# Moving the projection of the gated addend from the attention to the gate stage of a two-layer hybrid encoder

## The chip, the cores and the metric

One core of a Trainium2 chip runs the whole kernel. The metric is the device time of one execution in microseconds (us). PE is TensorE, DVE VectorE, ACT ScalarE, POOL GpSimd; SP is SyncE, which here issues every DMA.

## The reference

The kernel does one inference step of a two-layer encoder over 1024 prompt tokens and 64 sample tokens, T = 1088 columns here. Each layer projects the normalized input, runs three token mixers (latent attention with 8 heads, causal pooling, chunk-band attention with 4 heads), merges them with gates, projects out and adds to x. The part of interest is the last line of a layer, in which `ple` is an input of 256 channels that depends on nothing else in the layer:

```python
def trunk_layer(x, ple, ...):
    h = rmsnorm(x, norm_in)
    ...
    m = (gates[..., :D_MODEL] * (o_a @ w_o_mla)
         + gates[..., D_MODEL:2 * D_MODEL] * (o_b @ w_o_pool)
         + gates[..., 2 * D_MODEL:] * (o_c @ w_o_ca))
    x = x + m @ w_out

    x = x + jax.nn.sigmoid(rmsnorm(x, ple_norm) @ w_ple_gate) * (ple @ w_ple_proj)
```

Widths: D_MODEL 1024, `ple` 256, so the projection `ple @ w_ple_proj` gives 1024 channels for 1088 tokens.

## The kernel before, in words

Activations lie channels by tokens: 8 blocks of 128 channels, each cut into two halves of H = 544 tokens, and a half into two quarters of C = 272 columns, which is the width of a matmul. For precision each operand is split into a rounded part and its rest (`split`: ScalarE makes the first, DVE or POOL the second), and one product is three matmuls (`mm3`, L132 to L134).

A layer runs through these stages: the input projection (`gemm`, L404), the attention, first the 4 chunk heads (scores S at L1034, softmax on DVE and ACT, transposes pT at L891, weighted sums pv at L917 and L925), then the 8 latent heads (scores at L1105), the merge, the output projection, and the gate stage (`ple_pairs`, matmuls in `plain`, L372). `plain` takes each of 4 pairs of channel blocks (p and p + 4); for each block and each token half it sums 48 matmuls into one PSUM tile g, calls the pair's `out`, and then its `mid`.

The code is written in program order, which is a priority: at build time a scheduler with an estimated clock per engine puts an instruction that is ready ahead of others that are not, later code filling idle time. What stands in the kernel is the outcome: a fixed queue for each engine, taken in order, with semaphores between. The DMAs all stand in one such queue, SP's.

Beside the attention run generators that are advanced step by step as filler: `ple_proj` (the projection), `pool_branch` (the pooling mixer, tile pbm) and then `merge_bc` (the part of the merge that needs no latent heads, tile mps, multiplied out at L1424). `begin_beside` makes them and the list FIRST = (2, 2, 1) says how many steps of them stand ahead of the first head. `ple_proj` loads `p` and `wpp`, splits them, computes the projection into a PSUM tile pps of pool po, copies it on ScalarE (L1444) to a tile o, and stores o to a DRAM buffer pp_d. In the gate stage `load` reads pp_d back, and `out` takes the sigmoid of the normalized sum (L748, L752; for the first pair L751 scales a copy), multiplies (L754) and adds to x (L755).

## Time and profile before

| what | value |
|---|---|
| three runs | 2278.78, 2288.59 and 2279.34 us |
| median | 2279.34 us |
| the profiled execution | 2290.6 us |
| its span in the trace | 2288.8 us |
| PE busy | 2163.4 us, 95% of the span |
| DVE busy | 1743.5 us, 76% |
| ScalarE busy | 1176.3 us, 51% |
| GpSimd busy | 693.4 us, 30% |
| granted TensorE clock, mean | 0.976 of full |

The span is the time from the first to the last event of one execution on the core; the profiled execution is a little longer than its span, and longer than the median. Busy shares are means over stages of different kinds. In layer 0 the chunk heads run from about 572 to 685 us, the latent heads to 905, the merge to 969, the output projection to 1053 and the gate stage to 1155; in layer 1 the chunk heads from 1706 to 1816 and the gate stage from 2182 to 2283.

### The profile page before, as it was taken

Reading aid. Unit: us, or ns where it says so; the run is one execution under the profiler, and the core shown is the slowest. Engines: PE = TensorE matmul, PEld = TensorE weight load, DVE = VectorE, ACT = ScalarE, POOL = GpSimd, SP = SyncE. Lnnn points to the kernel's source line nnn. Section 1 sums busy time; section 2 is a strip of 40 time slices with the busy share of each in tenths; the row PEclk is TensorE's granted clock in tenths of the full one; section 3 lists DMA queues with packets and bytes.
Section 4 is the critical chain, followed back from the end, with each engine's and each line's share of the span. In section 5 each row is a group of like instructions: output and inputs, shape, how many; then the busy total and the mean of one; then the engine's idle time right before and its main releaser. Section 6 shows DMA issues by size and latency. Waiting matters only on the chain.

```text
span 2288.8 us, 44876 instructions
## 1 busy us (share of the span) xinstructions
PE 2163.4 (95%) x16326; PEld 2083.9 (91%) x16326; DVE 1743.5 (76%) x3590; ACT 1176.3 (51%) x2491; POOL 693.4 (30%) x918
## 2 busy tenths in 40 slices
PE   5999999999789999899989999999988899999998
PEld 4999999999588998899979999999987889998998
DVE  8777888676568889887686678876747788889764
ACT  6234455454667666335453343555546776653341
POOL 0000044676455554000000000547574665430000
PEclk8999999999899999999989999999999999999999
DMA  3534546455966764545634345554569666645472
GB/s 125 185 110 135 185 142 193 129 158 143 279 196 183 198 172 136 204 173 179 210 107 139 118 158 173 165 157 127 159 179 276 199 186 179 186 162 186 144 232 74
DMA packets 222191, 385.81 MB, mean 169 GB/s; under 512 B 30404, under 2 KB 114196, under 8 KB 221972
## 3 DMA queue, kind: packets, MB, share of 16 engines
q1 hardware_dynamic: 221972, 382.95, 54.2%
q8 instruction: 130, 2.13, 0.4%
q14 instruction: 89, 0.73, 0.1%
HBM read 248.16 MB, written 134.70 MB: 167 GB/s over the span
## 4 chain that ended last, share of the span: by engine, by line
PE 62%; DMA 15%; DVE 13%; ACT 4%; issue 3%; POOL 2%; SPq 1%; DVEq 0%; ACTq 0%; POOLq 0%
PE g L404 36%; PE g L372 6%; PE S L1105 3%; PE pv L925 3%; PE pT L891 3%; DMA pp<-o 3%; DMA g<-z 2%; PE mps L132 1%; DMA mb<-g 1%; SPq L87 1%; DVE wop L121 1%; DMA r<-rd 1%; PE mps L134 1%; PE mps L133 1%; PE vps L1074 1%
## 5 line engine op out<-in xcount | busy, mean ns | idle before, releaser
L110 ACT CAST wop<-wraw 128x512 fp32r<-128x512 f32 (+1 forms) x238 | 143.8, 606 | 259.3 <-PE g L404 154.8
L865 POOL TENSOR_SCALAR P<-P,st 128x640 f32<-128x640 f32 (+8 forms) x216 | 155.3, 723 | 203.0 <-DVE st L864 122.3
L121 POOL TENSOR_TENSOR wop<-wraw,wop 128x512 fp32r<-128x512 f32 (+1 forms) x80 | 99.3, 1244 | 382.9 <-ACT wop L110 382.4
L121 DVE TENSOR_TENSOR PT<-pT,PT 128x512 fp32r<-128x512 f32 (+4 forms) x360 | 167.6, 473 | 39.3 <-ACT PT L110 37.3
L121 DVE TENSOR_TENSOR wop<-S,wop 128x512 fp32r<-128x512 f32 x178 | 141.6, 795 | 68.1 <-ACT wop L110 67.6
L110 ACT CAST wop<-S 128x512 fp32r<-128x512 f32 x202 | 124.6, 618 | 123.4 <-PE g L404 119.6
L110 ACT CAST PT<-pT 128x512 fp32r<-128x512 f32 (+4 forms) x360 | 147.0, 420 | 54.4 <-PE pT L891 47.8
L404 PE MATMUL g<-B11h,wop 128*128 128x272 f32 x832 | 152.4, 294 | 16.5 <-ACT B11h L112 12.7
L925 PE MATMUL pv<-PT,V 128*128 128x256 f32 x928 | 165.4, 297 | 2.5 <-DVE PT L121 1.6
L1105 PE MATMUL S<-K,Q 96*128 96x384 f32 (+5 forms) x672 | 158.8, 353 | 6.5 <-ACT P L857 6.5
L132 PE MATMUL mps<-oh,wop 128*128 128x272 f32 x512 | 155.2, 304 | 8.6 <-DVE g L1424 3.9
L891 PE MATMUL pT<-ident,P 128*128 128x128 f32 x936 | 158.5, 279 | 2.9 <-DVE PT L121 1.2
L404 PE MATMUL g<-T3h,wop 128*128 128x272 f32 x832 | 153.9, 293 | 7.7 <-ACT T3h L110 5.0
L404 PE MATMUL g<-B21h,wop 128*128 128x272 f32 x832 | 156.3, 298 | 4.8 <-ACT P L416 4.6
L404 PE MATMUL g<-T1h,wop 128*128 128x272 f32 x832 | 151.7, 293 | 3.6 <-DVE z L681 1.9
L404 PE MATMUL g<-T2h,wop 128*128 128x272 f32 x832 | 152.9, 294 | 2.1 <-ACT T2h L110 1.8
L404 PE MATMUL g<-B22h,wop 128*128 128x272 f32 x832 | 151.0, 293 | 0.0
L404 PE MATMUL g<-T4h,wop 128*128 128x272 f32 x832 | 149.7, 291 | 0.0
L134 PE MATMUL mps<-oh,wop 128*128 128x272 f32 x512 | 148.3, 290 | 0.0
L857 ACT ACTIVATE P<-S,st 128x384 f32<-128x384 f32 (+5 forms) x224 | 126.7, 572 | 38.2 <-DVE st L853 27.1
L925 PEld LDWEIGHTS pv<-PT,V 128*128 128x128 f32 x928 | 131.1, 191 | 11.0 <-DVE PT L121 6.2
L404 PEld LDWEIGHTS g<-B11h,wop 128*128 128x128 f32 x832 | 124.0, 192 | 18.1 <-ACT B11h L112 13.2
(291 smaller groups left out, 6591.0 us busy)
## 6 DMA issues: line engine op xcount, KB each, us to landing
wraw<-win SPq DMA_DIRECT2D x88, 512.0 KB
z<-z SPq DMA_DIRECT2D x96, 272.0 KB
g<-z SPq DMA_DIRECT2D x64, 272.0 KB
z<-z SPq DMA_DIRECT2D x24, 544.0 KB
Q<-q SPq DMA_DIRECT2D x32, 408.0 KB
K<-k SPq DMA_DIRECT2D x32, 400.0 KB
k<-hl SPq DMA_DIRECT2D x48, 256.0 KB
q<-hl SPq DMA_DIRECT2D x64, 192.0 KB
```

What stands on the lines that cost most here:

```text
L87: self.nc.sync.dma_start(out=self.raw(out), in_=self.raw(in_))
L110: nc.scalar.copy(out, src)
L121: e.tensor_sub(out, src, hi)
L132: mm(ps, lhsT=wh, rhs=xh, start=first, stop=False)
L134: mm(ps, lhsT=wl, rhs=xh, start=False, stop=last)
L372: self.nc.tensor.matmul(ps[:, c, :C], lhsT=hl[kh][:, w, kb, :], rhs=b[:, kb, c * C:(c + 1) * C], start=kh + k == 0, stop=kh == 1 and k == 11)
L404: nc.tensor.matmul(ps[:, c, :C], lhsT=hl[:, w, kb, :], rhs=b[:, kb, c * C:(c + 1) * C], start=k == 0 and not more, stop=k == 11, skip_grou ...
L857: nc.scalar.activation(u.p[:, c * w:c * w + w], x, AF.Exp, bias=st[:, 0:1], scale=-1.0, accum_out=st[:, 2 + c:3 + c])
L865: nc.gpsimd.tensor_scalar(u.p[:, :n], u.p[:, :n], st[:, 4:5], 1.0, op0=ALU.mult, op1=ALU.mult)
L891: nc.tensor.transpose(ps[:, j], p[:, c0:c0 + 128], self.ident)
L925: nc.tensor.matmul(ps[:, :w], lhsT=v(b), rhs=grp[b // 4][:, b % 4, j, :w], start=i + j == 0, stop=i == len(bl) - 1 and j == 1)
L1105: nc.tensor.matmul(ps[:, :ww], lhsT=q[0:96, q0:q0 + 128], rhs=k[0:96, k0 + c * w:k0 + c * w + ww], start=i == 0, stop=i == 2 and not diag)
```

## The change

`ple_proj` and its DRAM buffer are gone. In the gate stage `addend` loads the four tiles of `p` and splits them into ph and pl, which stay for the stage; `load` does the same with each block's weights (wph, wpl). `out` now ends with the sigmoid, and `done`, called behind each block's 48 matmuls, computes the block's addend with 12 matmuls pps into PSUM of pool pn, multiplies the sigmoid by it straight from PSUM in two halves (L778) and adds to x (L780). The raw tiles of the loads are the two buffers of tag sq. In layer 0 the blocks of x that the next layer's norm needs are reloaded at other places. Only the first step of the pooling stands ahead of the first head. The core of the diff:

```diff
@@ -51,7 +51,7 @@
 LATE = 100
 NEAR, BESIDE = 8, 14
 PVE = ("v",)
-FIRST = (2, 2, 1)
+FIRST = 1
 OV = 0
 QC, QM = (8, 0, 1, 2, 3, 4, 5, 6, 7), (2, 3, 6, 7, 8, 0, 1, 4, 5)
 L1, L2 = 1, 5
@@ -132,6 +132,11 @@
         mm(ps, lhsT=wh, rhs=xh, start=first, stop=False)
         mm(ps, lhsT=wh, rhs=xl, start=False, stop=False)
         mm(ps, lhsT=wl, rhs=xh, start=False, stop=last)
+
+    def halve(self, hl, raw, src):
+
+        self.ld(raw, src)
+        self.split(raw, hl[0], hl[1])
 
     def pool(self, name, side="left", bufs=1, **kw):
         return self.tc.tile_pool(name=name, bufs=bufs, side=side, reuse_waits="tile", **kw)
@@ -224,7 +228,7 @@
         yield
         pt = self.pn.tile([128, 512], F32, tag="n", name="rT")
         nc.tensor.transpose(pt[:n, :128], r, self.ident)
-        rt = self.cp.tile([32, 128], F32, tag="rt", name="rt")
+        rt = self.cp.tile([32, 128], F32, tag="rt", name="rt", bufs=1)
         nc.vector.tensor_copy(rt[:n], pt[:n, :128])
         rd = self.dp.tile([ng, w], F32, name=f"rd{self.nr}")
         self.nr += 1
@@ -733,13 +737,24 @@
         nc, d = self.nc, self.d
         last = l == L - 1
         xo = d["y"] if last else self.xb_d[l]
-        x, pp = {}, {}
+        x, g, add, w = {}, {}, {}, {}
 
         def load(p):
             if p < 4:
                 order = (0, 0), (0, 1), (4, 0), (4, 1)
-                self.new_pair(pp, self.pp_d[l], p, order)
                 self.new_pair(x, self.xa_d[l], p, order)
+                for m in (p, p + 4):
+                    w[m] = tuple(self.xp.tile([128, 2, 128], F32R, tag=f"wp{s}", name=f"wp{s}", bufs=2) for s in "hl")
+                    raw = self.sv("sq").rearrange("p a c -> p (a c)")[:, :256].rearrange("p (k c) -> p k c", k=2)
+                    self.halve(w[m], raw, d["wpp"][l, m])
+
+        def addend():
+
+            for ti in range(2):
+                for k in range(2):
+                    add[k, ti] = tuple(self.xp.tile([128, H], F32R, tag="x", name=f"p{s}", bufs=NX) for s in "hl")
+                    raw = self.sv("sq").rearrange("p a c -> p (a c)")
+                    self.halve(add[k, ti], raw, d["p"][l, k][:, ti * H:ti * H + H])
 
         def out(p, mi, ti, op, ps, sb):
             m = p + 4 * mi
@@ -750,9 +765,19 @@
                 nc.scalar.copy(t, ps)
                 nc.vector.tensor_mul(t, t, self.half(self.r, ti))
             nc.scalar.activation(t, t, AF.Sigmoid)
-            g, o = self.halves(pp[m, ti]), self.halves(x[m, ti])
-            nc.vector.tensor_mul(g, g, t)
-            nc.vector.tensor_add(o, o, g)
+            g[m, ti] = t
+
+        def done(m, ti):
+
+            t = g.pop((m, ti))
+            for c in range(2):
+                cc = slice(c * C, c * C + C)
+                ps = self.pn.tile([128, 512], F32, tag="n", name="pps")
+                for k in range(2):
+                    self.mm3(ps[:, :C], w[m][0][:, k], w[m][1][:, k], add[k, ti][0][:, cc], add[k, ti][1][:, cc], k == 0, k == 1)
+                nc.vector.tensor_mul(t[:, c], t[:, c], ps[:, :C])
+            o = self.halves(x[m, ti])
+            nc.vector.tensor_add(o, o, t)
             if last:
                 self.st(xo[m][:, ti * H:(ti + 1) * H], x[m, ti])
             else:
@@ -761,22 +786,21 @@
         def begin(p):
             if p == 0:
                 self.plain_boundary(self.x, l, G_PLE)
+                addend()
                 load(0)
             load(p + 1)
 
-        def mid(j):
-            if not last and j == 1:
-                for kb in range(2):
-                    self.new_pair(self.x, xo, kb)
-            if not last and j == 2:
-                self.new_pair(self.x, xo, 2)
+        def mid(p, j):
+            done(p + 4 * (j // 2), j % 2)
+            if not last and p == 3 and j < 2:
+                self.new_pair(self.x, xo, j)
 
         def next_begin():
-            self.x.update({k: t for k, t in x.items() if k[0] % 4 == 3})
+            self.x.update({k: t for k, t in x.items() if k[0] % 4 > 1})
             self.norm_boundary(self.x, l + 1, G_IN)
 
         return [Pair(lambda kh, p=p: d["wpg"][l, p, kh], lambda *a, p=p: out(p, *a), lambda p=p: begin(p),
-                     mid if p == 3 else None, plain=True) for p in range(4)], next_begin
+                     lambda j, p=p: mid(p, j), plain=True) for p in range(4)], next_begin
 
 
     def attention(self, units, near, look=2):
@@ -825,12 +849,10 @@
             self.seq = HEADS
             self.vt, self.ot = {}, {}
             self.begin_beside(l)
-            self.advance(0, FIRST[0])
             self.load_head(0)
             self.sp = es.enter_context(self.pool("at", self.O))
             lay(self.sp, AT)
-            self.advance(0, FIRST[1])
-            self.advance(1, FIRST[2])
+            self.advance(0, FIRST)
             near = {}
             near.setdefault(BESIDE, []).append(lambda: self.beside(l))
             near.setdefault(NEAR, []).append(lambda: self.last_pairs(l))
@@ -1116,8 +1138,8 @@
     def begin_beside(self, l):
 
         es = self.bes = ExitStack()
-        e, p = (es.enter_context(self.pool(n, self.B, b)) for n, b in (("s2e", 2), ("s2p", 1)))
-        self.bg = [self.ple_proj(l, e, p), self.pool_branch(l, p)]
+        p = es.enter_context(self.pool("s2p", self.B, 1))
+        self.bg = [self.pool_branch(l, p)]
 
     def advance(self, i, n):
         for _ in range(n):
@@ -1427,25 +1449,6 @@
             self.ld(self.mb_d[l][m][:, ti * H:ti * H + H], gs[0])
 
         yield from self.ahead(sp, [self.mbo_d[l][0], self.mbo_d[l][1], self.o_d[l][0], self.o_d[l][1]], weights, work, gates)
-
-    def ple_proj(self, l, sp, op):
-        nc, d = self.nc, self.d
-
-        def weights(m):
-            return self.weights(d["wpp"][l, m], 2)
-
-        def work(ti, m, hl, w, _):
-            o = op.tile([128, H], F32, tag="po", name="o", bufs=2)
-            for c in range(2):
-                cc = slice(c * C, c * C + C)
-                ps = self.po.tile([128, 512], F32, tag="o", name="pps")
-                for k in range(2):
-                    self.mm3(ps[:, :C], w[:, 0, k], w[:, 1, k], hl[k][0][:, cc], hl[k][1][:, cc], k == 0, k == 1)
-                nc.scalar.copy(o[:, cc], ps[:, :C])
-            yield
-            self.ld(self.pp_d[l][m][:, ti * H:ti * H + H], o)
-
-        yield from self.ahead(sp, [d["p"][l, 0], d["p"][l, 1]], weights, work, els=("g", "v"))
 
 
     def last_pairs(self, l):
```

First PE, at the beginning of the chunk heads in layer 0. g is the tile of the last block of the input projection, pps the projection's PSUM tile with the split input oh, ol and the weights wop, S the scores of keys K and queries Q. Before:

```order
L404 MATMUL g_6792<-B22h_160,wop_6759 128x272 x2
L132 MATMUL pps_10172<-oh_6865,wop_6900 128x272
L133 MATMUL pps_10172<-ol_6866,wop_6900 128x272
L134 MATMUL pps_10172<-oh_6865,wop_6900 128x272
L132 MATMUL pps_10172<-oh_6894,wop_6900 128x272
L133 MATMUL pps_10172<-ol_6895,wop_6900 128x272
L134 MATMUL pps_10172<-oh_6894,wop_6900 128x272
L1034 MATMUL S_6926<-K00_6853,Q00_6854 128x288
L1034 MATMUL S_6926<-K00_6853,Q10_6855 128x288
L1034 MATMUL S_6930<-K00_6853,Q00_6854 128x288
L1034 MATMUL S_6930<-K00_6853,Q10_6855 128x288
L1034 MATMUL S_6948<-K00_6853,Q00_6854 128x128
```

and after:

```order
L408 MATMUL g_6790<-B22h_158,wop_6757 128x272 x2
L1056 MATMUL S_6896<-K00_6851,Q00_6852 128x288
L1056 MATMUL S_6896<-K00_6851,Q10_6853 128x288
L1056 MATMUL S_6900<-K00_6851,Q00_6852 128x288
L1056 MATMUL S_6900<-K00_6851,Q10_6853 128x288
L1056 MATMUL S_6918<-K00_6851,Q00_6852 128x128
L1056 MATMUL S_6918<-K00_6851,Q10_6853 128x128
L1056 MATMUL S_6927<-K00_6851,Q00_6852 128x256
L1056 MATMUL S_6927<-K00_6851,Q10_6853 128x256
L1056 MATMUL S_6949<-K00_6851,Q00_6852 128x384
L1056 MATMUL S_6949<-K00_6851,Q10_6853 128x384
L1056 MATMUL S_6974<-K00_6851,Q00_6852 128x512
```

The pps matmuls no longer stand between the scores, and the scores of head 0 follow one another (up to the pooling's first matmul, four rows further on). From the first chunk score to the first latent score PE's queue holds 556 matmuls before, 179 of them pps, and 397 after, with 15 mps and 9 pbm that stood later before, and 4 vps fewer.

Next PE in the gate stage of layer 0, where a block's sum ends with operand T4 and the next begins with B22. Before:

```order
L372 MATMUL g_13677<-T4h_11897,wop_13672 128x272 x4
L372 MATMUL g_13677<-T4l_11898,wop_13672 128x272 x2
L372 MATMUL g_13677<-T4h_11897,wop_13672 128x272 x4
L372 MATMUL g_13677<-T4l_11898,wop_13672 128x272 x2
L372 MATMUL g_13677<-T4h_11897,wop_13672 128x272 x2
L372 MATMUL g_13739<-B22l_11903,wop_13610 128x272 x2
L372 MATMUL g_13739<-B22h_11902,wop_13610 128x272 x4
L372 MATMUL g_13739<-B22l_11903,wop_13610 128x272 x2
```

and after:

```order
L376 MATMUL g_13883<-T4h_11539,wop_13839 128x272 x2
L132 MATMUL pps_13940<-ph_13163,wph_13543 128x272
L133 MATMUL pps_13940<-pl_13164,wph_13543 128x272
L134 MATMUL pps_13940<-ph_13163,wpl_13544 128x272
...
L132 MATMUL pps_13948<-ph_13169,wph_13543 128x272
L133 MATMUL pps_13948<-pl_13170,wph_13543 128x272
L134 MATMUL pps_13948<-ph_13169,wpl_13544 128x272
L376 MATMUL g_13961<-B22h_11544,wop_13763 128x272 x2
L376 MATMUL g_13961<-B22l_11545,wop_13763 128x272 x2
```

Behind the block's last T4 matmul now stand 12 pps matmuls (three products for each of two channel halves of p, and that for two quarters) and only then the next block. There are 16 such groups in each layer; the first stands some 180 gate matmuls behind the stage's begin.

Last DVE in the gate stage, for one block in the middle. Before:

```order
L748 TENSOR_TENSOR ev<-g,rbc 128x544
L121 TENSOR_TENSOR wop<-wraw,wop 128x512
L754 TENSOR_TENSOR x<-x,ev 128x544
L755 TENSOR_TENSOR x<-x 128x544
L455 TENSOR_TENSOR acc<-acc,sq 128x544
L748 TENSOR_TENSOR ev<-g,rbc 128x544
```

and after:

```order
L763 TENSOR_TENSOR ev<-g,rbc 128x544
L121 TENSOR_TENSOR wop<-wraw,wop 128x512
L778 TENSOR_TENSOR ev<-ev,pps 128x272 x2
L121 TENSOR_TENSOR wpl<-sq,wph 128x256
L780 TENSOR_TENSOR x<-x,ev 128x544
L345 TENSOR_TENSOR S_14491<-wraw 128x512
L459 TENSOR_TENSOR acc<-acc,sq 128x544
L345 TENSOR_TENSOR S_14493<-S_14491,wraw 128x512
L763 TENSOR_TENSOR ev<-g,rbc 128x544
```

One multiply of a whole half (L754) has become two of a quarter each, with PSUM as one operand (L778), and among them the low parts of the weights (wpl) are made.

## Rows read from the trace of the kernel before

**Rows 1.** Windows by stage: length, busy us of each engine, granted clock, DMA share.
```profile
core 0: us, PE busy (x) PEld busy (x) DVE busy (x) ACT busy (x) POOL busy (x), PEclk, DMA share, GB/s
572.00:685.00 113.00, 89.24 (x576) 79.46 (x575) 72.89 (x260) 72.17 (x202) 58.47 (x90) 0.91 0.86 237
685.00:905.00 220.00, 212.35 (x1595) 194.57 (x1594) 186.67 (x537) 149.46 (x439) 116.79 (x165) 1.00 0.62 178
1053.00:1155.00 102.00, 101.60 (x817) 101.27 (x817) 72.41 (x110) 49.11 (x78) 0.00 (x0) 1.00 0.61 203
1706.00:1816.00 110.00, 88.87 (x583) 79.20 (x582) 73.05 (x261) 72.56 (x205) 58.71 (x90) 0.92 0.87 245
```

**Rows 2.** The chunk stages' windows, tile pps alone: PE, weight load and ScalarE.
```profile
572.00:685.00 113.00, 35.35 (x183) 28.73 (x184) 11.51 (x30) 0.91 0.86 237
1706.00:1816.00 110.00, 34.80 (x185) 28.43 (x185) 11.50 (x30) 0.92 0.87 245
```

**Rows 3.** Waits of PE, 572 to 685: total us, times, longest us.
```profile
PE pps L132 <- ACT o L1444: 10.4, 6, 3.7
PE pps L132 <- ACT oh L110: 4.8, 1, 4.8
```

**Rows 4.** Waits of PE, 1706 to 1820.
```profile
PE pps L132 <- ACT o L1444: 9.3, 6, 2.8
PE pps L132 <- ACT oh L110: 5.9, 1, 5.9
```

**Rows 5.** Windows of short stretches of the chunk stage, columns as in Rows 1.
```profile
576.00:588.00 12.00, 5.17 (x23) 3.99 (x22) 6.10 (x14) 5.59 (x11) 6.70 (x6) 0.71 0.99 320
594.00:609.00 15.00, 13.26 (x90) 11.22 (x88) 11.96 (x54) 10.27 (x28) 6.85 (x14) 1.00 1.03 326
622.00:627.00 5.00, 0.63 (x3) 0.30 (x2) 1.56 (x6) 0.55 (x2) 1.20 (x3) 0.85 1.05 286
627.00:633.00 6.00, 6.00 (x29) 6.00 (x30) 2.35 (x8) 4.54 (x12) 2.54 (x4) 0.56 1.05 207
```

**Rows 6.** DMA traffic and issues, 572 to 685.
```profile
DMA packets 13612, 26.77 MB, mean 237 GB/s; under 512 B 2557, under 2 KB 6653, under 8 KB 13600
...
pp<-o SPq DMA_DIRECT2D x15, 272.0 KB
...
of<-p SPq DMA_DIRECT2D x2, 272.0 KB
```

**Rows 7.** Groups by line, the chunk scores: whole stage, then 594 to 609.
```profile
L1034 PE MATMUL S<-K,Q 128*128 128x320 f32 (+5 forms) x112 | 27.6, 347 | 3.1 <-DMA Q<-qc 1.4 <-DVE st L1036 1.3 <-DVE PT L121 0.4
...
L1034 PE MATMUL S<-K,Q 128*128 128x320 f32 (+5 forms) x24 | 5.9, 344 | 0.7 <-DMA Q<-qc 0.7
```

**Rows 8.** Timeline of PE, first and last gate matmuls of layer 0.
```profile
1054.31 0.41 PE L372 MATMUL g<-T3h,wop 128*128 128x272 f32 x2
...
1152.62 0.41 PE L372 MATMUL g<-T1h,wop 128*128 128x272 f32 x2
```

**Rows 9.** Window of the boundary behind layer 0's gate stage, columns as in Rows 1.
```profile
1155.00:1182.00 27.00, 17.06 (x89) 14.97 (x87) 26.76 (x43) 13.88 (x23) 0.00 (x0) 0.74 0.10 31
```

**Rows 10.** Timeline of DVE, the norm's row in the gate stage of layer 0.
```profile
1072.27 0.28 DVE L228 COPY rt<-rT 9x128 f32<-9x128 f32 x1 [1.63 <-PE rT L226]
...
1077.69 2.00 DVE L751 TENSOR_TENSOR ev<-ev,rbc 128x544 f32<-128x544 f32 x3 [3.67 <-DMA rbc<-rd]
```

**Rows 11.** Group by line, DVE's multiply of the merge from PSUM, 685 to 905.
```profile
L1424 DVE TENSOR_TENSOR g<-g,mps 128x272 f32<-128x272 f32 x61 | 26.1, 428 | 4.5 <-DMA g<-z 3.8 <-PE mps L134 0.3
```

**Rows 12.** Timeline of DVE, the last gate block of layer 1.
```profile
2282.73 0.72 DVE L748 TENSOR_TENSOR ev<-g,rbc 128x544 f32<-128x544 f32 x1 [2.98 <-PE g L372]
...
2284.23 0.73 DVE L754 TENSOR_TENSOR x<-x,ev 128x544 f32<-128x544 f32 x1 [0.78 <-ACT ev L752]
2284.99 0.72 DVE L755 TENSOR_TENSOR x<-x 128x544 f32<-128x544 f32 x1
```

More of the change, by code (lines that the diff above doesn't have):

```diff
@@ L179, in setup @@
         self.z_d = f("z", [NZ, 128, T])
-        self.pp_d = f("pp", [8, 128, T])
         self.mb_d = f("mb", [8, 128, T])
```

## The prediction

> **What bounds the kernel now.** The page comes first: TensorE (PE) is busy 95% of the span, VectorE (DVE) 76%, ScalarE 51%. A mean over stages says little of one stage, so I cut the span at the stages' borders and read busy time, granted clock and DMA share of each [rows 1]. In the stage of the latent heads PE works 212 of 220 us, and in the gate stage 101.6 of 102: there every matmul more or less is time. The stage of the chunk heads is the exception, once in each layer: PE works 89.2 of 113 us (88.9 of 110 in layer 1) at a granted clock of 0.91, DVE only 73, while the DMA engines are 86% busy. That is the stage which loses the projection. Next I split off the projection's tile, pps: 183 matmuls are 35.4 us of PE's 89.2 there, and its copies 11.5 us of ScalarE [rows 2]. Then PE's waits: of the 23.8 us that PE idles in the stage, 10.4 are pps waiting for a copy to clear its PSUM bank (L1444) and 4.8 one wait for the split of p; layer 1 has 9.3 and 5.9 [rows 3, 4]. So the projection is filler that now stops the engine it was to fill: PE takes its queue in order, and scores stand behind a stopped pps.
>
> **The change part by part.**
>
> *Out of the chunk stage.* In PE's order of instructions 179 pps matmuls leave the stretch between the first chunk score and the first latent one, and 18 others (15 mps of the merge among them) come in: 556 instructions become 397. What is left of PE's work is 89.2 - 35.4 = 53.9 us, less than DVE's 73 [rows 1, 2], so the new length can't be PE's work. Bounds: below, DVE's 72.9 us plus 1 us to begin, 74. Above, the bytes: 26.77 MB pass in the stage, of which 15 stores of 272 KB and 2 loads of p go, 17 x 0.2785 = 4.7 MB [rows 6]; 22.0 MB at the stage's own 237 GB/s are 93 us. Between them stands a stretch with nearly nothing but attention in it: from 594 to 609 PE ran at full clock and DVE was busy 12.0 of 15 us [rows 5], and 24 of the stage's 112 scores were done [rows 7]. At that pace 112 scores take 70 us. To it I add 12 for the start, in which PE now gets 5.2 us of work into 12 while the first keys, queries and values land [rows 5], and 1 for the second pool block, which now lies wholly in the stage: **83 us**. I take this value because it is a measured pace of the same instructions with the same bytes in flight (326 GB/s there), where the upper bound takes a mean over stretches in which PE was stopped by other things. Gain: 30 in layer 0 and 27 in layer 1, **-57**.
>
> *Clock.* After 5 us in which PE did 0.6 us of work, the next 6 us ran at a granted 0.56, and the stretch of the start at 0.71; full activity had 1.00 [rows 5]. The Trainium skill, "TensorE: Matmul & The Clock Gate", section "Loop structure matters more than you think", says that a wait for DMA between matmuls lets PE go cold. This trace agrees as far as the 0.56 behind the idle 5 us goes. The sum by the trace's pace keeps full clock; by the rule the stage could get slower than the pace says, and that is a rival below.
>
> *Latent stage.* 27 matmuls fewer stand in its queue (7 pps, 15 mps and 9 pbm that went ahead, 4 vps that came later). PE is full there, so each is worth its step of 0.125 us, which the gate stage shows (next part): 3.4 a layer, **-6.8**.
>
> *Into the gate stage.* 16 groups of 12 pps a layer, 192 matmuls of 128x272. The stage's matmuls have that shape: between 1054.3 and 1153.0 [rows 8] lie 768 of the gate and 19 small ones, 0.125 us each. PE idles 0.4 us there, so no hole hides them: 192 x 0.125 = 24.0 a layer, **+48**. DVE gets two half multiplies from PSUM in place of one from SBUF. The nearest row is the merge's L1424, the same shape from PSUM: 0.427 us [rows 11], so 0.85 in place of 0.73 [rows 12], 16 times, 2 us on an engine with 30 us of idle in the stage: hidden. The splits of p and of the weights (12 on ScalarE, 12 on DVE) hide in the same idle; if that cover fails, they cost what the next item says.
>
> *First group.* p (four tiles) and the weights pass through two raw buffers, and in SP's queue some of these loads stand ahead of the row store and load of the norm. No row of before shows such a wait. Below: nothing, since the first group stands 180 gate matmuls (22 us) into the stage. Above: the norm's row itself took 5.4 us from its copy to its use, with 3.67 of waiting for the load [rows 10]; something over that, 6. I take 2 a layer, being nearer to the end with 22 us of lead: **+4**.
>
> *Merge earlier.* 15 mps now stand inside the chunk heads, where the DMA engines are full, with their gates' loads. mps waits for its multiply (L1424) now and then; a stop like pps's single 4.8 us [rows 3] is the upper end, 6 with what stands behind, and 0 the lower. I take 1.5 a layer, **+3**.
>
> *Boundary.* Between the gate stage of layer 0 and the next projections DVE works 26.8 of 27 us [rows 9], so what is added on it there is time: 42 instructions instead of 38 from the last block's scaling to the norm chain, in DVE's order, at 0.7 us [rows 12], **+2.8** (0 to 5). At the very end, the block's sigmoid now runs beside the last 12 pps, and only 0.43 + 0.72 us [rows 11, 12] stand behind them instead of 3.0 [rows 12], and some 0.5 for the sigmoid's own end: **-1.3**.
>
> Gone without a price: store and reload of pp in DRAM, 32 x 272 KB each way; the copies (L1444) on ScalarE, which is half idle.
>
> Sum: -57 - 6.8 + 48 + 4 + 3 + 2.8 - 1.3 = -7.3 us, 2283.3 against the profiled execution's 2290.6 (span 2288.8). The median of the runs is 2279.3, 11.3 below that execution, so **2272.0** on its basis. The change trades 57 us of a stage with holes against 48 in one without; what is left is small beside the uncertainty of the 83.
>
> **The rivals.**
>
> *The chunk stage falls to DVE's work.* With no pps stopping PE, softmax never starves: 74 us a stage instead of 83. For it: nearly two thirds of PE's idle time were pps's waits, and the best stretch had DVE at 80% in spite of 11 pps in it. Against: the same stretch waits for loads now and then, and the start can't be pressed out. 18 us more gain: -25.3, **2254.0**.
>
> *The DMA engines are the bound of the chunk stage* (the other side). With its share at 0.86 to 0.87 over the stage and above 0.98 in every one of its short stretches [rows 1, 5], taking PE's work out only uncovers it: 93 us a stage gains 37 instead of 57. For it: the share; loads of the merge come in as p's and the stores go. Against: the same engines moved 326 GB/s from 594 to 609, and part of their load runs ahead for later heads. 20 more: +12.7, **2292.0**. From 86.7 us a stage on it decides: there the sum is zero.
>
> *The clock falls.* Without filler PE has 54 us of work in a stage of 80, and a lower granted clock as behind the idle 5 us [rows 5] (1.2 of 2.4 GHz is 0.5) doubles it: some 100 us with the dependencies between. For it: 0.56 and 0.71. Against: 1.00 in the stretch of almost pure attention. Gain only 23: +26.7, **2306**. The Trainium skill's page named above would have it so if the loads for each score are what PE waits on; the 3.1 us that scores waited [rows 7] speak against it.
>
> *The move hides in the gate stage.* If the 192 matmuls cost nothing there, the gain is 48 more, **2224**; PE's 0.4 us of idle speaks against it.
>
> **How the numbers follow.** Chances: forecast 0.48, DVE floor 0.25, DMA bound 0.18, clock 0.07, hidden 0.02. The forecast's own range is 2262 to 2283 (stage 80 to 87 and the waits' ends). A change under 0.5%, 11.4 us, can hardly be told from none in this kernel: that is 2267.9 to 2290.7. Faster: the floor's 0.25, 0.02, and a small part of the forecast, 0.33. Slower: the clock's 0.07, half of the DMA bound and some of the forecast's upper tail, 0.21. Same: 0.46. The range runs from the floor with no waits added (2254 - 7, 2247) to a little over the DMA bound (2297), with 0.2 outside.
>
> **What would show it.** Right: the stage of chunk heads at 80 to 87 us with PE at some 55 to 60 us of work and no wait of a pps in it; the gate stage at 124 to 128 with PE full; at most 6 us of idle ahead of the first pps. The forecast is wrong if the chunk stage stays over 90, its waits then being for K, Q or V, or if its granted clock is under 0.85; if the gate stage grows by much over 26 us, with PE waiting for wph, ph or the norm's row; or if the latent stage grows because the merge's filler was used up too early.

## The result

The changed kernel takes 2306.3 us (median of 4 runs, 2304.3 to 2307.8) against 2282.4 us before (4 runs, 2278.8 to 2288.6): a ratio of 1.0094, with an interval of 1.0077 to 1.0111. It is slower by some 24 us and lies 9 us above the upper end of the forecast range. The profiled execution of the change has a span of 2302.4 us, 13.6 us above the one of before; the rest of the difference is that the profiled execution of before was itself some 8 us over the median and that of the change 2 under its own.

Stage by stage (both profiled executions). The chunk heads run from their first score to the first latent one, the latent heads to their last score, the merge and output projection from there to the first gate matmul, and the gate stage to the start of its last gate matmul, so that its last 12 pps fall to what follows:

| stage | before | after | difference | in the sum |
|---|---|---|---|---|
| start and first projection | 575.6 | 574.0 | -1.6 | 0 |
| chunk heads, layer 0 and 1 | 109.7, 106.8 | 92.2, 95.8 | -28.5 | -57 and +3 |
| latent heads | 215.6, 215.3 | 214.5, 217.8 | +1.4 | -6.8 |
| merge and output projection | 153.4, 153.1 | 149.9, 150.9 | -5.7 | 0 |
| gate stage | 98.5, 98.3 | 126.2, 124.8 | +54.2 | +48 and +4 |
| boundary and second projection | 556.1 | 549.8 | -6.3 | +2.8 |
| end | 6.4 | 6.5 | +0.1 | -1.3 |

The differences add up to 13.6. The windows by stage of the changed kernel, columns as in [rows 1], to be read against it:

```profile
574.00:666.00 92.00, 70.88 (x404) 58.62 (x405) 66.91 (x254) 57.49 (x157) 50.50 (x79) 0.87 0.87 235
666.00:885.00 219.00, 211.11 (x1574) 192.70 (x1573) 186.91 (x540) 149.22 (x436) 113.32 (x163) 0.99 0.59 165
...
1030.00:1158.00 128.00, 124.80 (x982) 124.11 (x982) 78.20 (x135) 52.43 (x87) 0.00 (x0) 0.99 0.44 146
...
1706.00:1802.00 96.00, 70.57 (x402) 58.71 (x403) 66.73 (x255) 57.44 (x158) 50.29 (x79) 0.86 0.85 228
...
2170.00:2297.00 127.00, 124.85 (x986) 124.37 (x985) 60.76 (x109) 33.50 (x56) 0.00 (x0) 0.99 0.36 118
```

The gate stage is full before and after, only with 180 more matmuls between its ends. The chunk stage has lost 172 and 181 matmuls in these windows and ends up with about as many holes as before: PE idles 21 of 92 us where it idled 23.8 of 113. PE's waits there, with the same columns as [rows 3]:

```profile
PE S L1056 <- DVE st L1058: 9.9, 9, 6.6
PE mps L132 <- ACT oh L110: 3.5, 1, 3.5
PE S L1056 <- DVE z L690: 3.4, 1, 3.4
PE S L1056 <- DMA Q<-qc: 2.4, 2, 1.7
```

The waits of [rows 3] are gone. The largest wait that came, 6.6 us, lies at the start. Split there, the stage reads (same columns):

```profile
574.00:590.00 16.00, 8.73 (x29) 7.12 (x30) 7.78 (x27) 7.85 (x17) 8.23 (x12) 0.51 0.97 257
590.00:666.00 76.00, 62.15 (x377) 51.51 (x376) 59.13 (x228) 49.64 (x141) 42.27 (x67) 0.95 0.85 230
```

16 us pass until the heads run freely, at a granted clock of 0.51, about the lower of its two levels (1.2 of 2.4 GHz), and then 76 us in which neither PE nor DVE, ScalarE or GpSimd is full. The wait at the start is one of DVE, which stands for the pooling's sums of GpSimd while the first scores of head 0 are queued behind:

```profile
580.04 1.28 DVE L1365 SCALAR_TENSOR_TENSOR pl<-pb,pinv,pu 128x1024 f32<-128x1024 f32 x1 [6.12 <-POOL pb L1347]
```

A row of before that the prediction did not read turns out to be the main one. ScalarE's waits in the chunk stage of layer 0 of the kernel before (572 to 685; total us, times, longest):

```profile
ACT o L1444 <- DMA pp<-o: 13.8, 4, 5.4
```

The copy L1444 waits for a store of its own tile o to land before it may fill the tile again, and there are only two such tiles. The longest of these waits stops three engines (before, timelines of ScalarE, PE and DVE; in brackets the idle time just ahead and what ended it):

```profile
626.45 0.39 ACT L1444 COPY o<-pps 128x272 f32<-128x272 f32 x1 [5.39 <-DMA pp<-o]
626.89 0.59 PE L132 MATMUL pps<-oh,wop 128*128 128x272 f32 x1 [3.70 <-ACT o L1444]
627.68 0.16 DVE L864 RECIPROCAL st<-st 128x1 f32<-128x1 f32 x1 [4.07 <-ACT P L857]
```

ScalarE stands in the copy, the next pps of PE behind the copy, and DVE behind an exponential of the softmax (L857) that is in ScalarE's queue behind the copy. It is the stretch from 622 to 627 in which PE did 0.6 us of work [rows 5]; the 0.56 of the clock came behind it. The chain of what ended last in the stage names two more such stores (before; start, us, what):

```profile
633.45 9.88 DMA pp<-o
643.43 0.39 ACT o L1444
643.87 0.39 PE pps L132
...
657.72 10.00 DMA pp<-o
667.80 0.39 ACT o L1444
668.24 0.40 PE pps L132
```

A store takes 10 us there from its issue to its landing, among the other transfers.

### The profile page after: what moved, and what is told of

The parts are those of the page before. It is cut to its first block, busy times and chain, and to the rows that moved or that the text cites. A ratio compares the mean times of both kernels' runs of the same rounds, so it can differ in the third digit from the quotient of the medians.

```text
span 2302.4 us, 44709 instructions
## 1 busy us (share of the span) xinstructions
PE 2170.1 (94%) x16326; PEld 2084.4 (91%) x16326; DVE 1748.2 (76%) x3642; ACT 1160.3 (50%) x2427; POOL 677.5 (29%) x898
## 4 chain that ended last, share of the span: by engine, by line
PE 62%; DVE 14%; DMA 11%; issue 4%; ACT 4%; POOL 3%; SPq 1%; POOLq 0%; DVEq 0%; ACTq 0%
PE g L408 33%; PE g L376 6%; PE S L1127 4%; PE pv L947 4%; PE pT L913 3%; DMA Q<-qc 2%; DMA r<-rd 2%; DMA pu<-z 1%; PE mps L132 1%; DVE wop L121 1%; PE mps L134 1%; PE mps L133 1%; DMA of<-o 1%; PE vps L1096 1%; DMA of<-mbo 1%
## 5 line engine op out<-in xcount | busy, mean ns | idle before, releaser
L110 ACT CAST wop<-wraw 128x512 fp32r<-128x512 f32 x222 | 137.3, 620 | 266.2 <-PE g L408 150.2
L121 POOL TENSOR_TENSOR wop<-wraw,wop 128x512 fp32r<-128x512 f32 x64 | 85.8, 1345 | 368.8 <-ACT wop L110 368.5
L132 PE MATMUL mps<-oh,wop 128*128 128x272 f32 x512 | 155.7, 305 | 15.7 <-ACT oh L110 13.6
L947 PEld LDWEIGHTS pv<-PT,V 128*128 128x128 f32 x928 | 134.9, 198 | 24.5 <-DVE PT L121 10.4
L408 PE MATMUL g<-T4h,wop 128*128 128x272 f32 x832 | 149.2, 290 | 0.0
```

The lines of the kernel that those rows point to most:

```text
L110: nc.scalar.copy(out, src)
L121: e.tensor_sub(out, src, hi)
L132: mm(ps, lhsT=wh, rhs=xh, start=first, stop=False)
L408: nc.tensor.matmul(ps[:, c, :C], lhsT=hl[:, w, kb, :], rhs=b[:, kb, c * C:(c + 1) * C], start=k == 0 and not more, stop=k == 11, skip_grou ...
L947: nc.tensor.matmul(ps[:, :w], lhsT=v(b), rhs=grp[b // 4][:, b % 4, j, :w], start=i + j == 0, stop=i == len(bl) - 1 and j == 1)
```

## The experiments

Three theories of why the chunk stage is shorter by 14 us and not by 28. **A**: work on PE or DVE bounds it. **B**: the bytes bound it (the rival on the DMA engines, whose 93 us the stage had met). **C**, first stated beside the runs on the bytes: ScalarE standing in its copy until a store lands. Stage lengths below are worked out as in the table above, layer 0 and layer 1. The diffs are excerpts, long lines shortened with "...".

| run | ratio to before | interval | chunk heads | latent heads | gate |
|---|---|---|---|---|---|
| changed kernel | 1.0094 | 1.0077 to 1.0111 | 92.2, 95.8 | 214.5, 217.8 | 126.2, 124.8 |
| gate_no_pps | 0.9893 | 0.9869 to 0.9917 | 95.3, 97.5 | 215.0, 215.7 | 101.0, 99.5 |
| chunk_no_pps | 0.9990 | 0.9970 to 1.0009 | 106.1, 109.2 | 212.7, 214.5 | 98.4, 98.3 |
| chunk_no_pool | 1.0073 | 1.0046 to 1.0100 | 93.6, 95.1 | 215.8, 215.9 | 127.6, 125.7 |
| after_first0 | 1.0097 | 1.0065 to 1.0129 | 94.7, 94.8 | 213.2, 217.9 | 124.0, 124.1 |
| chunk_no_stores | 1.0030 | 1.0020 to 1.0041 | 107.0, 104.4 | 222.1, 220.1 | 98.4, 98.3 |
| after_stores | 1.0103 | 1.0086 to 1.0120 | 89.6, 92.9 | 221.8, 217.2 | 124.6, 123.2 |
| before_o6 | 0.9944 | 0.9927 to 0.9960 | 97.3, 96.8 | 223.7, 221.1 | 98.4, 98.3 |
| before_o6_f0 | 0.9949 | 0.9932 to 0.9966 | 99.8, 100.1 | 218.2, 219.8 | 98.5, 98.4 |
| after_copies2 | 1.0148 | 1.0130 to 1.0166 | 99.7, 99.3 | 218.0, 217.6 | 126.1, 124.1 |
| after_copies4 | 1.0096 | 1.0077 to 1.0115 | 91.8, 93.8 | 216.4, 217.6 | 124.6, 124.0 |
| before_o4 | 0.9998 | 0.9983 to 1.0013 | 101.4, 101.7 | 227.8, 222.9 | 98.4, 98.3 |
| after_matmuls | 1.0172 | 1.0144 to 1.0199 | 103.9, 100.6 | 213.9, 211.2 | 124.2, 123.4 |
| no_pps_o6 | 1.0028 | 1.0014 to 1.0043 | 113.3, 111.5 | 216.7, 214.4 | 98.4, 98.4 |

**What the matmuls cost in the gate stage** (gate_no_pps, from the changed kernel):

```diff
-                ps = self.pn.tile([128, 512], F32, tag="n", name="pps")
-                for k in range(2):
-                    self.mm3(ps[:, :C], w[m][0][:, k], ...)
-                nc.vector.tensor_mul(t[:, c], t[:, c], ps[:, :C])
+                nc.vector.tensor_mul(t[:, c], t[:, c], add[c, ti][0].bitcast(F32)[:, cc])
```

> The changed kernel without the 192 pps matmuls a layer in the gate stage; the sigmoid is multiplied by a slice of ph instead, so p is not projected. Loads and splits of p and wpp stay. Matmuls are the cost: the gate stage falls from 126.5 and 125.1 us (first to last gate matmul) to 100 to 103, and the time by 48 to 52 us, to about 2256. Loads, splits and the reordered reloads cost a good part: the gate stage stays at 108 or more, and the time falls by 40 or less. In both the chunk stages stay at 92 and 96 us.

The stage falls to 101.0 and 99.5 us and the time to 2259.8, 46.5 below the changed kernel. The matmuls (180 of the 192 lie between the stage's ends) are 25.2 and 25.3 us of the stage, and all the rest that came into it (loads, splits, the first group's wait) 2.5 and 1.2. The matmul cost is settled.

**PE's work in the chunk stage** (chunk_no_pps, from the kernel before):

```diff
-                ps = self.po.tile([128, 512], F32, tag="o", name="pps")
-                for k in range(2):
-                    self.mm3(ps[:, :C], w[:, 0, k], w[:, 1, k], ...)
-                nc.scalar.copy(o[:, cc], ps[:, :C])
+                nc.scalar.copy(o[:, cc], self.raw(hl[c][0][:, cc]))
```

> The kernel before without the 192 pps matmuls a layer beside the chunk heads; the copies take split p instead of PSUM, so p is not projected. Its loads, splits, copies and the stores of 272 KB stay. PE's stops were the cost (theory A): the chunk stages fall from 110 and 107 us to 92 to 98, and the time by 20 to 30 us, to about 2257. The DMA engines bound the stage (theory B): with all 26.8 MB still to move it stays at 104 or more, and the time falls by under 10 us.

The stages are 106.1 and 109.2 us and the time is that of before: taking the matmuls and their stops out gains nothing, where theory A had 20 to 30 us. But PE's work did not fall by 35 us with them. Window of layer 0's stage (columns as in [rows 1]):

```profile
573.00:680.00 107.00, 79.29 (x404) 64.42 (x405) 73.48 (x259) 73.36 (x200) 59.95 (x88) 0.78 0.95 273
```

PE is busy 79.3 us with 404 matmuls, where the 393 other than pps took 62.6 in before (worked out from the trace as the time in which at least one of them ran), and the granted clock is 0.78 instead of 0.91. So the run speaks against theory A as it stood, but cannot part it from a loss of clock; the test with more buffers, below, is the cleaner one.

**The pooling's arithmetic** (chunk_no_pool, from the changed kernel; everything between its loads and its store is left out):

```diff
-            a = sp.tile([128, W], F32, tag="pa", name="pa")
...
+            o = u[:, 16:1104]
+            yield
             self.ld(self.mbo_d[l][j], o)
```

> The changed kernel with the arithmetic of the pooling left out (its loads and its store of 544 KB a block stay, the store taking the loaded block). Theory A, the chunk stage is bound by the softmax chain on DVE and what is put between on DVE (13 us of pooling in the stage, and 6 us of waiting for GpSimd's sums ahead of head 0): the chunk stages fall from 92 and 96 us to 76 to 82, the time by 24 to 34 us. Theory B, the DMA engines: the bytes are the same, the stages stay at 89 or more, and the time falls by under 10 us.

93.6 and 95.1 us: some 10 us of DVE's work and 14 of GpSimd's less in the stage, and it is no shorter. DVE's work alone is thus not what sets its length. The wait at the start is another matter: the run has no such wait of DVE, but storing the loaded block itself made GpSimd wait for that store, with the softmax's scaling behind it in its queue, and PE stood 5.9 us for that instead:

```profile
583.30 0.11 POOL L1330 MEMSET pu<- 128x16 f32 x1 [8.95 <-DMA mbo<-pu]
```

What the pooling's place at the start costs is therefore not shown by this run.

**The first head's wait** (after_first0: FIRST = 0 in place of 1).

> The changed kernel with FIRST = 0: no step of the pooling stands ahead of the first chunk head. If DVE's 6.1 us wait for GpSimd's sums with the softmax of head 0 behind it is what delays the start, the chunk stages fall by 4 to 6 us each and the time by 8 to 12 us, to about 2296. If head 0 waits for its keys, queries and values anyway (theory B), the stages change by under 2 us, and the time by under 4.

94.7 and 94.8, and 2307.0 us: no change, but the edit did not take the wait out. The scheduler put the step in the same place, DVE stands there as before, and PE's scores wait 7.0 us for it:

```profile
580.25 1.28 DVE L1365 SCALAR_TENSOR_TENSOR pl<-pb,pinv,pu 128x1024 f32<-128x1024 f32 x1 [6.06 <-POOL pb L1347]
```

So the run says nothing on what the wait costs; that stays open.

**The bytes** (chunk_no_stores, from the kernel before; and after_stores, from the changed kernel):

```diff
-            self.ld(self.pp_d[l][m][:, ti * H:ti * H + H], o)
+            self.ld(self.pp_d[l][m][:, ti * H:ti * H + 16], o[:, :16])
```

```diff
+            if i < 32 and i % 2 == 0:
+                o = self.eo[i // 2 % 4]
+                nc.gpsimd.tensor_copy(o[:, :1], st[:, 4:5])
+                self.ld(self.pp_d[self.l][i // 4][:, ...], o)
```

> The kernel before with all its projection matmuls and copies beside the chunk heads, but each store of 272 KB cut to 16 of 544 columns (8 KB); the gate stage loads slices of p instead, of the same size, so the projection's result isn't used. Theory B, the DMA engines bound the chunk stage: 4.1 of 26.8 MB go, the stages fall from 110 and 107 us to 92 to 97 though PE keeps its 192 matmuls, and the time falls by 22 to 30 us, to about 2258. Theory A, PE and DVE bound it: the stages stay at 104 or more, the time falls by under 8.

> The changed kernel with 16 stores of 272 KB put back into each chunk stage, of four dummy tiles that are written once, a column of each touched by GpSimd to tie a store to a softmax unit; nothing is copied by ScalarE for it and nothing is reloaded. Theory B: 4.4 MB more at the stage's 235 GB/s, the stages grow from 92 and 96 us to 104 to 112, and the time by 24 to 34 us, to about 2335. Theory C, the stores cost only because the copies on ScalarE waited for the two buffers they leave from: no copy waits here, the stages stay under 99, and the time grows by under 8.

Theory B falls twice. With the stores cut to 8 KB and 4.1 MB less to move, the stages are 107.0 and 104.4 us, not 92 to 97, and the time is 2289.3, no shorter (the latent heads are 6.5 and 4.8 us longer; why, no run shows). And with 16 stores put back into the changed kernel the stage is not longer (89.6 and 92.9) and the time the same (2306.7), though layer 0's latent heads take 7 us more; the DMA engines move the added bytes in the same time. The traffic of layer 0's chunk stage, first the changed kernel (574 to 666), then after_stores (574 to 668):

```profile
DMA packets 8346, 21.60 MB, mean 235 GB/s; under 512 B 1924, under 2 KB 2959, under 8 KB 8335
```

```profile
DMA packets 10985, 26.71 MB, mean 284 GB/s; under 512 B 2192, under 2 KB 3498, under 8 KB 10974
```

The 235 GB/s were what was asked for, not what could be had. The share of 0.87 is a mean of 0.99 up to 654 us and 0.06 behind, where the stage still runs for 12 us; with the stores the first 80 us move 284 GB/s instead of 268. And in chunk_no_stores, with stores of 8 KB, the copies still waited for them (ScalarE's waits, 574 to 684):

```profile
ACT o L1444 <- DMA pp<-o: 7.3, 3, 4.0
```

Here a small store, too, landed late among large transfers. This is why theory C was tested by buffers.

**Joined loads** (after_wide and before_wide, from each kernel):

```diff
-        for i, p in enumerate((slice(0, 64), slice(64, 128))):
-            self.ld(k[p], self.kc_d[l][j, i][r])
-            self.ld(q1[p], self.qc_d[l][j, 0][r])
-            self.ld(q2[p], self.qc_d[l][j, 1][r])
+        self.ld(k, self.kc_d[l][j][:, r])
+        self.ld(q1, self.qc_d[l][j, 0][r][None].to_broadcast([2, 64, T]))
+        self.ld(q2, self.qc_d[l][j, 1][r][None].to_broadcast([2, 64, T]))
```

> The changed kernel with the loads of the chunk heads' keys and queries joined: a tile of 128 partitions comes in one DMA instead of two of 64 partitions, the same bytes from the same places. The DMA engines show about 200 GB/s in stretches of these loads and about 400 in others at the same full share. If loads of 64 partitions are the slow ones and the stage is bound by DMA (theory B), 5.7 MB a stage gain some 14 us: chunk stages of 78 to 85, and 20 to 30 us less, about 2280. If the width of a load doesn't matter, the stages stay within 3 us and the time within 6.

> The kernel before with the same joined loads. Theory B with narrow loads slow: chunk stages from 110 and 107 us to 94 to 99, and 20 to 30 us less, about 2258, the fastest of all so far. Otherwise the time stays within 6 us of before.

Both missed by far: ratios of 1.1105 and 1.1015, chunk stages of 181 to 191 us. The joined load, whose outermost dimension is 2, runs at some 53 GB/s with a DMA share of a tenth in the stretches where nothing else moves. The Trainium skill, "DMA: Bandwidth & Descriptors", section "Why a DMA increments its semaphore by 16 and not by 1", says that a DMA is spread over the largest number of engines, up to 16, that divides the slowest dimension of both its sides; by that it is 2 of 16 here. The share of a tenth agrees. So the test of narrow loads says nothing on width, which stays open.

**Theory C: more buffers** (before_o6, from the kernel before; before_o6_f0 has FIRST = (0, 0, 1) besides; before_o4 has 4):

```diff
-            o = op.tile([128, H], F32, tag="po", name="o", bufs=2)
+            o = op.tile([128, H], F32, tag="po", name="o", bufs=6)
```

> The kernel before with six buffers instead of two for the tile o from which the projection's result is stored; matmuls, copies, loads and stores are all there. Theory C, the chunk stages lose to ScalarE standing in its copy L1444 until an earlier store of the same buffer has landed, 8 to 10 us in a full DMA queue, with the softmax's exponentials queued behind it: those waits (13.8 us in layer 0) go, the stages fall from 110 and 107 us to 93 to 100, and the time by 18 to 30 us, to about 2258. Theory A, PE's own work of 35 us in the stage: no change beyond 4 us a stage, and the time within 8 of before.

The chunk stages fall by 12.4 and 10.0 us with all matmuls, copies and bytes in them, where theory A had at most 4, and the time to 2272.4 us, faster than both kernels. Windows of its two chunk stages, then PE's waits for pps in the first (columns as before):

```profile
571.00:669.00 98.00, 84.55 (x581) 76.95 (x582) 70.53 (x256) 70.60 (x199) 56.58 (x87) 0.93 1.01 288
1693.00:1790.00 97.00, 83.80 (x580) 75.73 (x580) 69.92 (x255) 71.29 (x200) 55.80 (x85) 0.95 1.00 293
```

```profile
PE pps L132 <- ACT oh L110: 6.0, 1, 6.0
PE pps L133 <- DVE ol L121: 1.5, 2, 0.9
PE pps L132 <- ACT o L1444: 1.1, 3, 0.5
```

The 10.4 us of pps waiting for the copy [rows 3] are 1.1 now, and ScalarE's wait for pp<-o is no longer in its list. The time fell by 12, not by the 22 that the stages gave: the latent heads are 8.1 and 5.8 us longer. A part of that is their filler, the merge, which had moved up to inputs that were not there yet (before_o6, PE's waits, 668 to 893; the same wait was 2.5 us in before):

```profile
PE mps L132 <- DVE g L1424: 6.8, 3, 5.3
```

> The same six buffers, and FIRST = (0, 0, 1): no step of the projection stands ahead of the first chunk head, so its loads and splits don't delay the head's softmax on DVE. If the 3 us of splits and the wait ahead of them (582 to 585 us before) count, another 3 to 5 us a stage come off, to about 2250; if the head waits for its values anyway, nothing.

No further gain: 2273.7 us, with chunk stages of 99.8 and 100.1.

> The kernel before with four buffers for o. A store lands 8 to 10 us after its issue, and a buffer is filled every 3 us or so where the projection runs freely: four buffers cover most of it. Theory C: chunk stages of 96 to 103 us, between those with two buffers (110, 107) and six (97, 97), nearer to six, and a time of 2270 to 2277.

The stages fall to 101.4 and 101.7 as expected, the time doesn't (2281.4): the latent heads take 12.2 and 7.6 us more, and there too PE waits for the merge's inputs (4.7 us for oh, where before had 0.9).

**Theory C from the other side** (after_copies2 and after_copies4, from the changed kernel: after_stores with a tile filled by ScalarE, and 2 or 4 tiles in turn):

```diff
+                o = self.eo[i // 2 % 2]
+                for c in range(2):
+                    nc.scalar.copy(o[:, c * C:c * C + C], st[:, 4:5].to_broadcast([128, C]))
```

> The changed kernel with 16 stores of 272 KB in each chunk stage as in the run with stores put back, but their tiles are now filled by two ScalarE copies of 128x272 each, tied to a softmax unit, and there are two tiles in turn. No matmul is added. Theory C: ScalarE waits for stores again, the chunk stages grow from 92 and 96 us to 103 to 115, and the time by 20 to 35 us, to about 2330. Without theory C only the copies' 12 us of work on a ScalarE that is 62% busy are added: the stages stay under 99.

> The same with four tiles in turn: the copies' work is the same, the waits for a store to land are mostly gone. Theory C: the chunk stages are within 5 us of the changed kernel's 92 and 96, and at least 8 us a stage below those with two tiles. If the copies' work itself is what costs, there is no difference between two tiles and four.

99.7 and 99.3 us with two tiles, 91.8 and 93.8 with four, by the same copies and the same bytes; a ratio of 1.0148 against 1.0096. The growth with two tiles, 7.5 and 3.5 us, is less than theory C expected (103 or more) and just over the 99 that stood for none; what decides is the difference between the two runs, 7.9 and 5.5 us a stage and 13.6 us of time. ScalarE's wait for the store in layer 0's chunk stage, two tiles and then four:

```profile
ACT o L894 <- DMA pp<-o: 10.3, 5, 3.2
```

```profile
ACT o L894 <- DMA pp<-o: 3.1, 2, 2.5
```

The wait costs, and the copies' own work costs nothing that can be seen: with four tiles the time is that of the changed kernel.

**The matmuls alone put back** (after_matmuls, from the changed kernel: `ple_proj` of before beside the heads, without its copies and stores, its result unused).

```diff
-        self.bg = [self.pool_branch(l, p)]
+        self.bg = [self.ple_proj(l, e, p), self.pool_branch(l, p)]
```

> The changed kernel with the projection's loads of p and wpp, its splits and its 192 matmuls put back beside each layer's chunk heads, without copies and stores (their result is not used; the gate stage still does the projection). If the matmuls fill holes of PE there (theory C's other half), the chunk stages are 92 to 99 us and the time is 4 to 12 us above the changed kernel's 2306. If each costs its 0.125 us, the stages are 112 or more and the time is 40 us above.

The chunk stages grow by 11.7 and 4.8, the latent heads shrink by 0.6 and 6.6, and the time is 2322.3 us, some 16 above the changed kernel. Both lie between the two expectations (stages of 92 to 99 or over 112, 4 to 12 us or 40), nearer to the first. Loads, splits and matmuls together cost 5 us a layer by the stages of the profiled execution and 8 by the time; in the gate stage the matmuls alone cost 25.

**A miss of theory C** (no_pps_o6: the edits of chunk_no_pps and of before_o6 together).

> The kernel before without the projection's matmuls (as in the run without pps matmuls, the copies taking split p), and with six buffers for o. Theory C: its waits were the store waits, which came earlier as nothing paced the copies; chunk stages fall from 106 and 109 us to 88 to 97. If something else held that run up (the splits, the copies' own 12 us, the clock at 0.78), they stay at 102 or more.

113.3 and 111.5 us, longer than with two buffers. The edit did not take the store waits out: ScalarE waits 5.2 us for them in layer 0's stage, and 3.9 in chunk_no_pps, too little to be why that run was no shorter. Its window of layer 0's chunk stage shows the granted clock at 0.79, PE without work for a third of the time, and the other matmuls taking 77.5 us as in chunk_no_pps:

```profile
571.00:684.00 113.00, 77.51 (x405) 65.34 (x406) 69.39 (x257) 71.99 (x199) 59.52 (x88) 0.79 0.92 257
```

In its chain of waits stand transfers of 8 to 13 us for keys, the pooling's gate and the latent keys. Without the matmuls between them the copies and stores stand elsewhere in the queues; which of clock, order and transfers makes the length stays open.

## Why the prediction was wrong

**Out of the chunk stage: the step that failed.** It says "At that pace 112 scores take 70 us" and adds 12 for the start: 83 us a stage, a gain of 57. Measured: 92.2 and 95.8, a gain of 28.5. Three things were wrong in it. First, the borders: the 113 and 110 from which the 83 was taken are windows that begin some 3 us ahead of the first score (575.6 and 1708.9), while the 83 counts from the first score. From score to score the stages took 109.7 and 106.8, so that 83 was worth 50.5 us and not 57; 6.5 of the missing 28.5 are this alone. Second, the start: 16 us in layer 0 instead of 12, with 6.6 of waiting behind the pooling's sums, which the stretch it was read from did not have. Third, the pace: 76 us for the rest, at no waits of pps, instead of 70 and 1. The best 15 us of the stage were taken for its pace. Read by whole heads (from the first score of one to the first of the next, 28 scores each, worked out from PE's timeline) the changed kernel's layer 0 takes 21.6, 21.8, 24.1 and 24.8 us a head; and before took 24.0, 22.2, 33.1 and 30.5, with the projection in it. The first two heads of the kernel before were thus only 2.4 and 0.4 us longer, with 36 and 24 pps among them, and the trace of before showed their length.

PE's work left was wrong too: "53.9 us" takes the whole 35.4 of pps off, which runs in part over other matmuls. Without pps it was 62.6 in before, and with 15 mps and 9 pbm more and a clock of 0.87 it measured 70.9. The sum did not use the 53.9, but it made PE's share of the stage look smaller than it is.

What sets the 76 us is not shown. The bytes do not (after_stores), nor does DVE's work (chunk_no_pool). The chain that ended last in the changed stage names three loads of 9 to 12 us each (after; start, us, what), while PE itself waits for loads of queries only 2.4 us:

```profile
596.39 8.82 DMA pu<-z
606.36 11.97 DMA Q<-qc
644.65 10.90 DMA of<-o
```

No run changed how late such a load lands and nothing else.

**The cause put on PE's waits.** The prediction read 10.4 us of pps waiting for a copy [rows 3] as the price of the projection in that place. It was in the main the price of two buffers. before_o6 takes 12.4 and 10.0 us off with the projection where it was, so of the 17.5 and 11.0 that the change gained only some 5 and 1 are left for the projection's matmuls, copies and splits; after_matmuls makes them 5 to 8 a layer with the latent heads counted. The matmuls whose work was to leave the stage were filler in holes for the most part, and the holes stayed: 21 us of 92.

**Into the gate stage.** Right in mechanism: 25.2 and 25.3 us where 24.0 was forecast, though with only 180 of the 192 between the stage's ends (gate_no_pps). PE's waits for pps in the stage were 2.8 us in layer 0 and 1.8 in layer 1, with 2 taken for each. Together 54.2 for 52.

**Latent heads and the merge.** -6.8 was forecast, and the stages came out at +1.4: in layer 0 there are 23 matmul records fewer (1561 to 1538 between the stage's ends) and it is 1.1 us shorter, in layer 1 it grew by 2.5 at a granted clock of 0.98. The merge's matmuls that went ahead stopped PE for 3.5 us in layer 0's chunk stage and 5.6 in layer 1's, one wait each, where 1.5 was taken; that is within its bounds of 0 to 6.

**Boundary.** +2.8 was forecast and -6.3 was measured over the boundary and the second projection together; the merge and output stages gave another 5.7. No run takes these apart, and a part is scatter: with no edit there, six other runs of the kernel before (those without joined loads) took 552.4 to 556.2 us for the boundary with the second projection and 149.2 to 153.1 for the merge and output stages, and seven of the changed one 547.0 to 553.4 and 149.8 to 151.7.

**The rivals.** The DMA rival's 93 us came true (92.2 and 95.8; its gain of 37 us did not, for the same borders), and its mechanism did not: after_stores shows 5 MB more in the stage with the stage no longer. A length that agrees is no proof of the reason. The floor at DVE's work did not come: DVE is busy 66.9 of the 92 us, and chunk_no_pool, with 10 us less of it, is no shorter. The clock rival's change of +26.7 us is near the measured +24 by luck: its stages of some 100 us and its clock of one half did not come, and other terms made up the rest. It has a part that no run singles out: 0.87 and 0.86 granted in the new chunk stages against 0.91 and 0.92 [rows 1], with 0.51 in the first 16 us and 0.95 behind them. Where the matmuls alone were taken out of the kernel before (chunk_no_pps, no_pps_o6) the clock is 0.78 to 0.80 and the rest of PE's work some 15 us longer; where they were put back into the changed kernel (after_matmuls) the clock rose from 0.86 to 0.93 in layer 1 and the stage was longer all the same. No run changes the clock by itself.

Range and chances: a 0.21 chance stood on slower, and the range, which ended a little over the DMA bound, was 9 us short. Against the sum, 25.5 us were lost in the chunk stages, 8.2 in the latent heads, 2.2 in the gate and 1.4 at the end, and 16.4 came back at the boundary (9.1), in the merge and output stages (5.7) and at the start (1.6): 20.9 in all, from -7.3 to +13.6.

## What to carry to other kernels

Before work is moved off a busy stage because an engine waits in it, ask what the awaited instruction waits for in turn: here PE waited for a ScalarE copy, the copy for a store of one of two buffers, and four more buffers gained 12 us where the move lost 24. Filler in a stage where PE has holes cost here a fraction of what it cost in a full one (5 to 8 of 25 us). Take a pace from whole periods of the loop (a head), never from its best stretch, and measure the old and the new length between the same borders. Look in the trace of each test whether the edit took the wait out that it was meant to: three tests here did not, or put another in its place.

## What the runs showed of the hardware that was not expected

- A mean DMA share of 0.87 at 235 GB/s in the changed kernel's chunk stage was not the limit of the DMA engines: with 5.1 MB more they moved 284 GB/s in the same time (after_stores), and 288 in before_o6. A full share did not mean one rate either: 268 GB/s at 0.99 in the changed kernel's first 80 us, 284 at 1.03 with the stores.
- Stores of 8 KB held up their buffers for up to 4.0 us in the full stage (chunk_no_stores), against up to 5.4 for stores of 272 KB.
- One load whose outermost dimension is 2, in place of two loads of 64 partitions, ran at about 53 GB/s (after_wide) where the same stage otherwise moved 235; the kernel became 11% slower. The traffic of 574 to 700 in that run, DMA engines' share in tenths and GB/s by 40 slices of 3.15 us:

```profile
DMA  1137451294971111111469981457411111115337
GB/s 50 53 117 232 101 169 53 76 302 150 274 270 55 53 53 53 49 53 53 139 184 276 231 231 50 140 194 237 175 53 53 58 54 55 53 53 144 122 90 237
DMA packets 7245, 15.88 MB, mean 126 GB/s; under 512 B 1701, under 2 KB 3493, under 8 KB 7239
```
